# A first stage that reads its features by rows from memory, with wider transfers and paired gate matmuls, in a one-core hybrid mLSTM / mixture-of-experts kernel

## Chip, cores and metric

The kernel runs on one core of a Trainium2 chip. The metric is the device time of one execution in microseconds (us); the time before is a median of three runs. PE is TensorE, DVE is VectorE, ACT is ScalarE, POOL is GpSimd, and SP is SyncE, which here only issues transfers.

## What is computed

One layer on 256 latent tokens and 256 context tokens of width 2048. The part that the change touches is the start of the mixer: LayerNorm, a modulation by shift and scale, and the first columns of the input projection.

```python
cond = silu(concat([c, c_ctx]))                       # two conditioning rows
mod  = cond @ w_ada + b_ada                           # 6 x 2048 for each row
hl = LN(x)   * (1 + scale_l) + shift_l                # latent tokens
hc = LN(ctx) * (1 + scale_c) + shift_c                # context tokens
q, k, v, i, f, o, u, bg, cg = split(hl @ w_in)        # latent: all columns
k, v, i, f of the context   = split(hc @ w_in[:, :state])
# bidirectional chunked mLSTM (context state, then latent) | short gated convolution
x1 = LN(alpha * x + gate * (concat(m, y) @ w_out)) * g1 + b1
# router, 16 SwiGLU experts (top 2), x = LN(alpha * x1 + gate * moe) * g2 + b2
```

## The kernel before

All large weights stream from memory once, in slabs of about 1 MB that SP issues one after another into a rotation of slots (`slab`, L125). A matmul of the mixer is three matmuls (`mm3`, L134): each operand is split into a rounded part (`..._hi`, `wq..h`) and a remainder (`..._lo`, `wq..l`), the rounded part by ACT (L281, L316), the remainder by DVE (L282, L317).

The stages follow one another: (1) the start, in which four row tiles `xrow` (two of the context, two of the latents) are loaded, DVE takes their LayerNorm statistics (`ln_stats`), DVE and ACT norm the rows (L255, L257), and PE transposes them by 128x128 blocks into `xT` (L269, copied out by L270); (2) a loop over 16 feature tiles j (L291) that accumulates q and k of the latents (`qps`, `kps`), k of the context (`kcps`) and the gates (`gps`); (3) the values (`vps`, weights `wv`), during which DVE also reduces 56 slabs `wt` of w_ada against the broadcast conditioning row `cbc` (L424); (4) the mLSTM and its projections, the output projection, the second norm and the router; (5) 16 experts, each with 24 slabs `we` (L909, L937).

In the loop of stage 2, feature tile j needs four numbers for each of its features, `mod`. `modulation(j)` makes them: 16 matmuls `ada` on two 1 MB slabs `wa` (L236), a DVE copy `part` (L239), two small matmuls that add the four partial rows up (L241) and a DVE addition (L244). ACT then makes `hm` = xT * scale + shift (L314, context half and latent half), `hc_hi` and `hl_hi` (L316) and the rounded weights (L281); 18 matmuls of 512 columns follow on PE, and two gate matmuls of 256 columns for this j (L330). The code calls `modulation(j + 2)` in loop j. In j = 10 to 13, 16 matmuls with `condf` against the identity spread the conditioning row over the partitions (L305), and DVE copies it to `cbc` (L307).

The order on each engine is fixed when the program is built: a scheduler takes the instructions of the code above and lists them for each engine, and each engine runs its list in that order, waiting where an operand isn't there.

Of the kernel before, what the change touches and what calls it, by code (L numbers as in the profile page):

```python
# [19 lines left out]
P = 128  # L20
# [35 lines left out]
ROT = 6  # L56
# [40 lines left out]
def tile_layer(ctx: ExitStack, tc: tile.TileContext, x, ctxt, condT, wada01, wadaT, wada5, b5, wqkg, wv, wproj,  # L97
# [9 lines left out]
    ringp = ctx.enter_context(tc.tile_pool(name="ringp", bufs=4))  # L107
# [3 lines left out]
    def mmt(name):  # L111
        return ps.tile([P, 512], F32, tag="mm", bufs=4, name=name)
# [4 lines left out]
    def adt(name):  # L117
        return ps.tile([P, 512], F32, tag="ad", bufs=1, name=name)

    slots = [(ringp, "ring")] * 4  # L120
# [80 lines left out]
    xT = xtp.tile([P, 16, 2 * T], F32, name="xT")  # L201
    rows = []
    for src in (ctxt, x):
        for tt in range(2):
            r = xp.tile([P, D], F32, tag=f"x{len(rows)}", name=f"xrow{len(rows)}")
            nc.sync.dma_start(r, src[tt * P:(tt + 1) * P, :])
            rows.append(r)
    nc.sync.dma_start(cst, consts)
    nc.sync.dma_start(sm, small)
# [10 lines left out]
    mods = {}  # L220
    wqs, was = {}, {}

    def load_ada(j):
        for hf in range(2):
            was[j, hf] = slab(f"wa{j}_{hf}")
            nc.sync.dma_start(was[j, hf], wada01[j, hf])

    def modulation(j):

        pa = adt(f"ada{j}")  # L230
        for hf in range(2):
            ws = was.pop((j, hf))
            wv_ = ws.rearrange("p (a n) -> p a n", a=8)
            for i in range(8):
                g = i % 4
                nc.tensor.matmul(pa[32 * g:32 * g + 32, 0:256], condf[:, hf * 8 + i, :], wv_[:, i, :],  # L236
                                 start=(hf == 0 and i < 4), stop=(hf == 1 and i >= 4), tile_position=(0, 32 * g))
# [8 lines left out]
    def load_qkg(j):  # L246
        wqs[j] = slab(f"wq{j}")
        nc.sync.dma_start(wqs[j][:, 0:1056], wqkg[j])

    load_ada(0)  # L250
    load_qkg(0)
    for i, r in enumerate(rows):
        mv, y, nb = ln_stats([r], f"l0_{i % 2}")
        if i > 1:
            nc.vector.tensor_scalar(r, r, y[:, 0:1], nb[:, 0:1], op0=ALU.mult, op1=ALU.add)  # L255
        else:
            nc.scalar.activation(r, r, AF.Identity, scale=y[:, 0:1], bias=nb[:, 0:1])  # L257

    bias4 = cp.tile([P, 16, 4], F32, name="bias4")
    for i in range(2):  # L260
        nc.vector.tensor_copy(bias4[:, :, i], sm[:, B_ADA:B_ADA + 16])
        nc.vector.tensor_scalar(bias4[:, :, 2 + i], sm[:, B_ADA + 16:B_ADA + 32], 1.0, None, op0=ALU.add)
    modulation(0)
    for i, r in enumerate(rows):
        for b in range(4):
            pt = mmt(f"xT{i}_{b}")
            for q in range(4):
                dt = b * 4 + q
                nc.tensor.transpose(pt[:, q * P:(q + 1) * P], r[:, dt * P:(dt + 1) * P], ident)  # L269
            (nc.vector.tensor_copy if b % 2 else nc.scalar.copy)(  # L270
                xT[:, b * 4:b * 4 + 4, i * P:(i + 1) * P], pt.rearrange("p (q t) -> p q t", q=4))
    load_ada(1)
# [3 lines left out]
    slots = slots + [(xp, f"x{i}") for i in range(4)]  # L276
# [13 lines left out]
    token_tiles(0)  # L290
    for j in range(16):  # L291
        if j + 2 < 16:
            load_ada(j + 2)
        if j + 1 < 16:
            load_qkg(j + 1)
        if j == 5:
            slots = [q for q in slots if q not in early]
            turn[0] = ROT
        if j == 8:
            token_tiles(1)  # L300
        if j in (10, 11, 12, 13):
            cb = adt(f"cb{j}")
            for q in range(4):
                k = (j - 10) * 4 + q
                nc.tensor.matmul(cb[:, q * P:(q + 1) * P], condf[:, k, 0:1].to_broadcast([P, P]), ident,  # L305
                                 start=True, stop=True)
            nc.vector.tensor_copy(cbc[:, (j - 10) * 512:(j - 9) * 512], cb)  # L307
        mod = mods.pop(j)
        wq = wqs.pop(j)
        jj, jt = j // 8, j % 8  # L310
        hm = cp.tile([P, 2, T], F32, tag="modt", bufs=2, name=f"hm{j}")
        for src, hi, lo, k in ((xT[:, j, 0:T], hc_hi, hc_lo, 1), (xT[:, j, T:2 * T], hl_hi, hl_lo, 0)):
# [5 lines left out]
        wh, wl = split(wq[:, 32:1056], [P, 1024], f"wq{j}")  # L318
# [386 lines left out]
    slots = [(endp, "N0"), (endp, "N1"), (endp, "N2"), (post, "W4")] + slots[i:] + slots[:i]  # L705
# [472 lines left out]
def pack(x, c, ctx, c_ctx, w_ada, b_ada, w_in, b_igate, b_fgate, mh_norm_g, conv_w, conv_b, w_out, ln1_g, ln1_b,  # L1178
# [33 lines left out]
    return [x, ctx, condT, wada01, wadaT, wada5, A(b_ada)[:, 10240:11264], wqkg, wv, wproj, wo, w1s, w3s, A(w2)[0], w2l, wrt,  # L1212
# [3 lines left out]
NAMES = ["x", "ctxt", "condT", "wada01", "wadaT", "wada5", "b5", "wqkg", "wv", "wproj", "wout", "w1", "w3", "w2", "w2l", "wrt",  # L1216
# [15 lines left out]
```

## Time and profile before

| | us |
|---|---|
| median of 3 runs | 1570.54 (1570.5 to 1570.57) |
| the profiled execution, its own time | 1572.7 |
| its span, first to last instruction | 1569.4 |
| PE busy in the span | 1435.5 (91%) |
| DVE busy | 557.6 (36%) |
| ACT busy | 347.1 (22%) |
| bytes moved by DMA | 585.52 MB, 373 GB/s on average |

The page lists, for the one profiled execution, each engine's busy time, and groups of equal instructions with the idle time ahead of them and what ended it. The times of single instructions and the waits come from queries of the same trace.

### The profile page before, as it was taken

The page shows a single profiled execution, that of the slowest core. Times are in us where ns is not written, and L with a number is a line of the kernel's source. Part 1 is how long each engine was busy: PE and PEld are TensorE (multiplying, and loading weights), DVE is VectorE, ACT ScalarE, POOL GpSimd, SP SyncE. Part 2 cuts the span into 40 slices and gives each one's busy share as a digit, 9 for nine tenths or more (in the row PEclk, how much of TensorE's full clock was granted, in tenths as well). Part 3 has the DMA queues.
Part 4 walks back from the last instruction along what each step waited for, and adds up shares of the span by engine and source line. Part 5 has one row for each costly group of instructions (what it writes and reads, how often), then busy time and mean ns, then how long its engine had stood idle before and what let it go on. Part 6 is the DMA issues. An engine that isn't in the chain of part 4 may idle for free. (4 is left out here: it accounts for less than half of the span.)

```text
span 1569.4 us, 19076 instructions
## 1 busy us (share of the span) xinstructions
PE 1435.5 (91%) x7917; PEld 800.3 (51%) x7917; DVE 557.6 (36%) x934; ACT 347.1 (22%) x600; POOL 9.7 (1%) x19
## 2 busy tenths in 40 slices
PE   5999999999999989999989989979879979889985
PEld 4666788999998855334324324324324324224331
DVE  6334986988876763110110110101101101101106
ACT  5333325644443342002002002002002002002101
POOL 0000000000000000000000000000000000000001
PEclk9999999999999989999999999999999999999998
DMA  9796796888878897999999999999999999999993
GB/s 393 295 389 266 272 397 238 314 327 324 318 297 325 299 400 306 422 421 422 421 422 421 422 422 421 422 422 421 422 422 421 421 421 422 422 409 413 420 377 134
DMA packets 84081, 585.52 MB, mean 373 GB/s; under 512 B 9636, under 2 KB 10904, under 8 KB 14232
## 3 DMA queue, kind: packets, MB, share of 16 engines
q1 hardware_dynamic: 82088, 579.96, 90.9%
q0 software_dynamic: 432, 3.15, 0.5%
q10 hardware_dynamic: 1472, 1.16, 0.3%
q8 instruction: 63, 1.03, 0.3%
q14 instruction: 26, 0.21, 0.0%
HBM read 582.06 MB, written 2.17 MB: 372 GB/s over the span
## 5 line engine op out<-in xcount | busy, mean ns | idle before, releaser
L909 PE MATMUL h<-we,xg 128*64 128x512 f32 x2048 | 460.2, 597 | 26.8 <-DMA we<-w 26.8
L909 PEld LDWEIGHTS h<-we,xg 128*64 128x64 f32 x2048 | 146.5, 137 | 313.1 <-issue 232.1
L937 PE MATMUL y<-we,aT 128*64 128x512 f32 x960 | 222.2, 600 | 39.4 <-DMA we<-w 28.5
L922 DVE TENSOR_TENSOR act<-act,h 128x512 f32<-128x512 f32 x16 | 11.0, 687 | 542.3 <-PE h L909 542.3
L937 PEld LDWEIGHTS y<-we,aT 128*64 128x64 f32 x960 | 62.3, 136 | 189.7 <-issue 88.5
L424 DVE CUSTOM_DVE_ANT_0 wt<-wt,cbc 128x2048 f32<-128x2048 f32 x56 | 127.3, 2284 | 9.2 <-DMA wt<-wadaT 9.1
L941 DVE TENSOR_TENSOR ysb<-y,g2b 128x512 f32<-128x512 f32 x30 | 20.7, 691 | 262.7 <-PE y L937 262.7
L875 ACT ACTIVATE xg<-gx,modc 128x128 f32<-128x128 f32 x127 | 55.7, 456 | 181.5 <-PE gx L871 178.3
L949 PE MATMUL cb<-ysb,pg 64*128 64x512 f32 x240 | 82.9, 635 | 0.0
L952 DVE TENSOR_TENSOR xl<-xl,cb 128x512 f32<-128x512 f32 x112 | 70.7, 682 | 5.5 <-PE cb L949 5.0
L919 ACT ACTIVATE pg<-pgp 128x256 f32<-128x256 f32 x16 | 6.1, 383 | 270.1 <-PE pgp L916 270.1
L871 PEld LDWEIGHTS gx<-oh,xh 128*128 128x128 f32 x512 | 59.4, 196 | 6.1 <-DVE xl L952 5.3
L871 PE MATMUL gx<-oh,xh 128*128 128x128 f32 x512 | 60.9, 281 | 0.7 <-DVE oh L850 0.7
L949 PEld LDWEIGHTS cb<-ysb,pg 64*128 64x128 f32 x240 | 31.0, 184 | 51.7 <-DVE xl L952 29.0
L927 ACT ACTIVATE aT<-atp 128x512 f32<-128x512 f32 x16 | 9.6, 597 | 214.0 <-PE atp L925 214.0
L921 ACT ACTIVATE act<-h 128x512 f32<-128x512 f32 x16 | 9.6, 597 | 139.1 <-PE h L909 139.1
L314 ACT ACTIVATE hm<-xT,mod 128x256 f32<-128x256 f32 x32 | 17.6, 595 | 74.1 <-DVE mod L244 74.1
L236 PE MATMUL ada<-wa,condf 128*32 128x256 f32 x512 | 31.8, 383 | 0.0
L239 DVE COPY part<-ada 128x256 f32<-128x256 f32 x16 | 6.8, 423 | 61.1 <-PE ada L236 61.1
L282 DVE TENSOR_TENSOR wo_0l<-wo,wo_0h 128x1024 fp32r<-128x1024 f32 x16 | 19.5, 1221 | 14.3 <-ACT wo_0h L281 14.3
L282 DVE TENSOR_TENSOR wo_1l<-wo,wo_1h 128x1024 fp32r<-128x1024 f32 x16 | 19.6, 1223 | 13.4 <-ACT wo_1h L281 13.4
L269 PE MATMUL xT<-cst,xrow 128*128 128x128 f32 x64 | 9.9, 314 | 15.1 <-DMA cst<-consts 14.7
(1123 smaller groups left out, 2221.2 us busy)
## 6 DMA issues: line engine op xcount, KB each, us to landing
we<-w SPq DMA_DIRECT2D x373, 1024.0 KB, 19.8
wt<-wadaT SPq DMA_DIRECT2D x56, 1024.0 KB, 7.1
wa<-wada SPq DMA_DIRECT2D x32, 1024.0 KB, 14.8
wo<-wout SPq DMA_DIRECT2D x16, 1024.0 KB, 7.0
wq<-wqkg SPq DMA_DIRECT2D x16, 528.0 KB, 13.7
wv<-wv SPq DMA_DIRECT2D x8, 1024.0 KB, 7.0
pu<-wproj SPq DMA_DIRECT2D x8, 1024.0 KB, 7.9
pc<-wproj SPq DMA_DIRECT2D x8, 1024.0 KB, 7.0
```

What stands on the lines that cost most here:

```text
L236: nc.tensor.matmul(pa[32 * g:32 * g + 32, 0:256], condf[:, hf * 8 + i, :], wv_[:, i, :], start=(hf == 0 and i < 4), stop=(hf == 1 and i >= ...
L282: nc.vector.tensor_sub(lo, w_ap, hi.bitcast(F32))
L314: nc.scalar.activation(hm[:, 1 - k, :], src, AF.Identity, scale=mod[:, 2 + k:3 + k], bias=mod[:, k:k + 1])
L424: nc.vector.tensor_tensor_reduce(ws, ws, cbc, 1.0, 0.0, ALU.mult, ALU.add, accum_out=adac[:, i:i + 1])
L871: nc.tensor.matmul(gp[:, i * n:(i + 1) * n], xh[t][:, dt * P:(dt + 1) * P], ohs[t], start=(t == 0), stop=(t == 1))
L875: nc.any.tensor_scalar(xg[:, dt, 0:n], gp[:, i * n:(i + 1) * n], sc2[:, dt:dt + 1], sh2[:, dt:dt + 1], op0=ALU.mult, op1=ALU.add)
L909: nc.tensor.matmul(h_[g * 64:g * 64 + 64, :], xs[:, dt, :], ws[:, c0:c0 + 512], start=(dt == 0), stop=(dt == 15), tile_position=(0, 64 * g))
L922: nc.vector.tensor_tensor(act, act, hp[1], op=ALU.mult)
L937: nc.tensor.matmul(yp[i][g * 64:g * 64 + 64, :], half(aT, ft), ws[:, c0:c0 + 512], start=(ft == 0), stop=(ft == 7), tile_position=(0, 64 * g))
L941: nc.vector.tensor_tensor(ysb[:, i * 512:(i + 1) * 512], yp[i], g2b[:, i * 512:(i + 1) * 512], op=ALU.mult)
L949: nc.tensor.matmul(cps, pg[gsl, t, :], ysb[gsl, i * 512:(i + 1) * 512], start=True, stop=True, tile_position=(64 * g, 0))
L952: nc.vector.tensor_tensor(acc[t][:, c0:c0 + 512], acc[t][:, c0:c0 + 512], cps, op=ALU.add)
```

## The change

Stage 1 and the loop of stage 2 are rebuilt; what follows them keeps its code, except for the pools from which its slots come.

- The four row tiles are still loaded, but only for the statistics. The features are loaded a second time in transposed order (`xTs`, four chunks of 1 MB, the first one in two pieces), and the program norms them there: `rnorm` and `bnorm` hold scale and offset of all 512 tokens in every partition (8 matmuls against the identity), and `normalise` multiplies and adds with two DVE instructions for each pair of feature tiles. The 64 transposes, their 16 copies and the four norms by row are gone.
- `wa` comes in 16 transfers of 2 MB into three wide slots, the weights of q and k in eight transfers of 1 MB for two j each (the first one in two halves), the gate columns of all j in one transfer `wg` of 0.26 MB.
- `modulation` is cut in two; in the code, `modulation_sums(j + 2)` (16 matmuls and the copy) stands between the halves t = 0 and t = 1 of the 18 matmuls, and `modulation(j + 2)` behind them.
- The gate matmuls of two j run together at the odd one.
- The conditioning row is loaded broadcast from memory (`crow`, 1 MB) and one ACT instruction applies SiLU; the 16 matmuls and four copies are gone.
- `hm` has three buffers instead of two. The ring of four 1 MB slots is opened behind the loop, in the place of the wide slots; for the experts it is closed and opened again with seven slots, which take the place of the four and of three others.

```diff
+    nc.sync.dma_start(cst, consts)
...
-    early = [(lat, "L1"), (lat, "L3"), (ctxp, "C1"), (ctxp, "C3")]
-    slots = slots + early
+    def load_xT(c):
+        xTc[c] = xtp.tile([P, 4, 2 * T], F32, tag=f"xT{c % 3}", name=f"xT{c}")
+        xv = xTs[c].rearrange("p (k t) -> p k t", k=4)
+        for k in ((0, 1), (1, 4)) if c == 0 else ((0, 4),):
+            nc.sync.dma_start(xTc[c][:, k[0]:k[1], :], xv[:, k[0]:k[1], :])
...
+    wide_slots = [(widep, "wa"), (widep, "wa"), (xp, "xA")]
+    pair_slots = [(lat, "L1"), (lat, "L3"), (ctxp, "C1"), (ctxp, "C3"), (xp, "x2"), (xp, "x3"), (xp, "x2"), (xp, "x3")]
...
-    def modulation(j):
+    def modulation_sums(j):
         pa = adt(f"ada{j}")
+        wv_ = was.pop(j).rearrange("p (a n) -> p a n", a=16)
+        for i in range(16):
+            g = i % 4
+            nc.tensor.matmul(pa[32 * g:32 * g + 32, 0:256], condf[:, i, :], wv_[:, i, :],
+                             start=(i < 4), stop=(i >= 12), tile_position=(0, 32 * g))
...
+    parts[j] = pa, part
+    def modulation(j):
+        pa, part = parts.pop(j)
...
+    rp_, bp_ = mlt("rnormp"), mlt("bnormp")
     for i, r in enumerate(rows):
...
+        for o, col in ((rp_, y), (bp_, nb)):
+            nc.tensor.matmul(o[:, i * P:(i + 1) * P], col[:, 0:1].to_broadcast([P, P]), ident, start=True, stop=True)
...
-                nc.tensor.transpose(pt[:, q * P:(q + 1) * P], r[:, dt * P:(dt + 1) * P], ident)
...
+    def normalise(j0, j1):
+        v = xTc[j0 // 4][:, j0 % 4:j0 % 4 + j1 - j0, :]
+        for row, op in ((rnorm, ALU.mult), (bnorm, ALU.add)):
+            nc.vector.tensor_tensor(v, v, row[:, None, :].to_broadcast([P, j1 - j0, 2 * T]), op=op)
...
     for j in range(16):
+        load_ada(j + 4)
+        if j % 2 == 0:
+            load_qk(j // 2 + 2)
...
+            nc.sync.dma_start(cbc, crow.to_broadcast([P, D]))
...
-        if j in (10, 11, 12, 13):
-            cb = adt(f"cb{j}")
...
+            if t == 0 and j + 2 < 16:
+                modulation_sums(j + 2)
         if j + 2 < 16:
             modulation(j + 2)
...
+        if j % 2:
+            for a in range(2):
+                for k in (j - 1, j):
...
+    wide.close()
+    ring = ExitStack()
+    ringp = ring.enter_context(tc.tile_pool(name="ringp", bufs=4, reuse_waits="tile"))
```

PE of the kernel before, from the last matmuls of j = 3 (`wq3`) to the first of j = 4 (`wq4`):

```order
L136 MATMUL kcps1_343<-wq3l_543,hc_hi0_347 128x512
L137 MATMUL kcps1_343<-wq3h_542,hc_lo0_348 128x512
L236 MATMUL ada5_564<-wa5_0_529,condf_70 32x256 x8
L236 MATMUL ada5_564<-wa5_1_531,condf_70 32x256 x8
L241 MATMUL ada5_564<-cst_69,part5_581 128x2 x2
L330 MATMUL gps_344<-hm4_595,wq4_533 32x256 x2
L135 MATMUL qps0_338<-wq4h_602,hl_hi0_345 128x512
```

The sums `ada5` stand behind the matmuls of j = 3, one whole j ahead of the first reader of `hm5`. PE of the changed kernel, from the last matmuls of j = 4 to the first of j = 5:

```order
L134 MATMUL kcps1_267<-wq4l_522,hc_hi0_271 128x512
L135 MATMUL kcps1_267<-wq4h_521,hc_lo0_272 128x512
L257 MATMUL ada5_474<-wa5_331,condf_67 32x256 x16
L267 MATMUL ada5_474<-cst_66,part5_491 128x2 x2
L366 MATMUL gps_268<-hm5_570,wg_101 32x256
L366 MATMUL gps_268<-hm4_514,wg_101 32x256
L366 MATMUL gps_268<-hm5_570,wg_101 32x256
L133 MATMUL kcps0_266<-wq5h_577,hc_hi0_271 128x512
```

The sums `ada5` have moved behind the matmuls of j = 4, directly ahead of the readers of `hm5`. ACT of the kernel before around the same place:

```order
L314 ACTIVATE hm4_595<-xT_86,mod4_525 128x256 x2
L316 ACTIVATE hc_hi0_347<-hm4_595 128x256
L316 ACTIVATE hl_hi0_345<-hm4_595 128x256
L281 ACTIVATE wq4h_602<-wq4_533 128x1024
L314 ACTIVATE hm5_655<-xT_86,mod5_585 128x256 x2
```

One j is one period of this list. ACT of the changed kernel, j = 4 and 5 (`wq2_275` is the slab of this pair):

```order
L342 ACTIVATE hm4_514<-xT1_122,mod4_447 128x256 x2
L344 ACTIVATE hc_hi0_271<-hm4_514 128x256
L344 ACTIVATE hl_hi0_269<-hm4_514 128x256
L311 ACTIVATE wq4h_521<-wq2_275 128x1024
L311 ACTIVATE wq5h_577<-wq2_275 128x1024
L342 ACTIVATE hm5_570<-xT1_122,mod5_504 128x256 x2
```

The rounded weights of both j of a pair stand behind `hl_hi` of the even one. SP of the kernel before, from the last slab `wa` to the first slabs of the values:

```order
L226 DMA wa15_1_1153<-wada01 128x2048
L248 DMA wq14_1155<-wqkg 128x1056
L248 DMA wq15_1217<-wqkg 128x1056
L445 DMA wv0_0_1372<-wv 128x2048
L423 DMA wt0_1430<-wadaT 128x2048
```

Two slabs of q and k follow the last `wa`. SP of the changed kernel at the same place:

```order
L238 DMA wa14_865<-wada01 128x4096
L249 DMA wq7_867<-wqk 128x2048
L238 DMA wa15_921<-wada01 128x4096
L484 DMA wv0_0_1248<-wv 128x2048
L462 DMA wt0_1306<-wadaT 128x2048
```

`wv0_0` now follows `wa15` directly; its slot lies in the place of a wide slot, and the transfer waits for the sums `ada15` on PE.

## Rows read from the trace of the kernel before

**Rows 1.** The page: the span, and the costliest group with the idle time before it

```profile
span 1569.4 us, 19076 instructions
...
L909 PE MATMUL h<-we,xg 128*64 128x512 f32 x2048 | 460.2, 597 | 26.8 <-DMA we<-w 26.8
```

**Rows 2.** Table of stretches: from:to, length, busy time by engine, granted clock, DMA

```profile
core 0: us, PE busy (x) PEld busy (x) DVE busy (x) ACT busy (x) POOL busy (x), PEclk, DMA share, GB/s
28.40:154.50 126.10, 119.67 (x912) 80.58 (x908) 45.58 (x86) 42.68 (x79) 0.00 (x0) 1.00 0.81 323
154.50:556.00 401.50, 399.60 (x2470) 356.43 (x2471) 319.68 (x446) 175.90 (x262) 0.97 (x6) 1.00 0.82 312
570.00:585.00 15.00, 8.77 (x88) 5.80 (x80) 9.34 (x34) 12.08 (x27) 0.00 (x0) 0.77 0.99 395
600.00:610.00 10.00, 10.00 (x65) 5.83 (x65) 5.78 (x26) 6.21 (x12) 0.00 (x0) 1.00 0.17 43
610.00:1505.00 895.00, 810.47 (x3826) 307.14 (x3824) 106.77 (x165) 78.45 (x167) 1.78 (x3) 1.00 1.01 418
```

**Rows 3.** What PE waited for, 28 to 560: total us, times, longest

```profile
PE ada L241 <- DVE part L239: 5.5, 10, 0.5
PE gtp L406 <- DVE tokt L397: 0.8, 1, 0.8
```

**Rows 4.** Timeline of PE, j = 2 to 3: start, length, instruction, [idle before]

```profile
46.90 0.50 PE L135 MATMUL qps<-wq2h,hl_hi 128*128 128x512 f32 x1
...
51.30 1.93 PE L236 MATMUL ada<-wa,condf 128*32 128x256 f32 x32
53.79 0.61 PE L241 MATMUL ada<-cst,part 128*128 128x2 f32 x4 [0.55 <-DVE part L239]
54.32 0.62 PE L330 MATMUL gps<-hm,wq 128*32 128x256 f32 x4
54.88 0.50 PE L135 MATMUL qps<-wq3h,hl_hi 128*128 128x512 f32 x1
```

**Rows 5.** Timeline of ACT at the same place

```profile
54.63 1.10 ACT L314 ACTIVATE hm<-xT,mod 128x256 f32<-128x256 f32 x2 [5.33 <-DVE mod L244]
55.63 0.40 ACT L316 ACTIVATE hc_hi<-hm 128x256 fp32r<-128x256 f32 x1
55.94 0.40 ACT L316 ACTIVATE hl_hi<-hm 128x256 fp32r<-128x256 f32 x1
56.24 1.05 ACT L281 ACTIVATE wq4h<-wq 128x1024 fp32r<-128x1024 f32 x1
```

**Rows 6.** Timeline of DVE at the same place

```profile
53.31 0.42 DVE L239 COPY part<-ada 128x256 f32<-128x256 f32 x1 [4.47 <-PE ada L236]
54.43 0.16 DVE L244 TENSOR_TENSOR mod<-ada,bias 128x4 f32<-128x4 f32 x1 [0.70 <-PE ada L241]
54.51 1.23 DVE L282 TENSOR_TENSOR wq3l<-wq,wq3h 128x1024 fp32r<-128x1024 f32 x1
```

**Rows 7.** PE where stages begin: j = 0, 10, 14, and the values

```profile
28.46 0.49 PE L135 MATMUL kcps<-wq0h,hc_hi 128*128 128x512 f32 x1
...
110.22 1.16 PE L305 MATMUL cb<-cst,condf 128*128 128x128 f32 x8
...
145.23 0.50 PE L135 MATMUL qps<-wq14h,hl_hi 128*128 128x512 f32 x1
...
155.17 0.50 PE L135 MATMUL vps<-wv_0h,hc_hi 128*128 128x512 f32 x1 [0.70 <-ACT qk_sb L359]
```

**Rows 8.** Timeline of DVE in the start

```profile
5.72 2.47 DVE L178 BATCH_NORM_STATS2 l_0st<-xrow 128x6 f32<-128x512 f32 x4 [5.72 <-DMA xrow<-ctxt]
...
18.65 1.34 DVE L255 TENSOR_SCALAR xrow<-xrow,l_0y,l_0nb 128x2048 f32<-128x2048 f32 x1
...
21.24 0.15 DVE L182 SCALAR_TENSOR_TENSOR l_1nb<-l_1mv,l_1y 128x1 f32<-128x1 f32 x1
```

**Rows 9.** The page's DMA issues: KB each, median us from issue to landing

```profile
wa<-wada SPq DMA_DIRECT2D x32, 1024.0 KB, 14.8
```

More of the change, by code (lines that the diff above doesn't have):

```diff
@@ L199, in token_tiles @@
         hc_lo.append(ctxp.tile([P, 8, T], F32R, tag=f"C{2 + i}", name=f"hc_lo{i}"))
[L201 to L209, printed above, removed]
     splits = ExitStack()
@@ L213, in tile_layer @@
     cbp = splits.enter_context(tc.tile_pool(name="cbp", bufs=1))
-    early = [(lat, "L1"), (lat, "L3"), (ctxp, "C1"), (ctxp, "C3")]
-    slots = slots + early
+    wide = ExitStack()
+    widep = wide.enter_context(tc.tile_pool(name="widep", bufs=2))
+    nc.sync.dma_start(cst, consts)
+    rows = []
+    xA = xp.tile([P, 2, D], F32, tag="xA", name="xrowA")
+    for i, src in enumerate((ctxt, x)):
+        for tt in range(2):
+            r = xA[:, tt, :] if i == 0 else xp.tile([P, D], F32, tag=f"x{2 + tt}", name=f"xrow{2 + tt}")
+            nc.sync.dma_start(r, src[tt * P:(tt + 1) * P, :])
+            rows.append(r)
@@ L219, in tile_layer @@
+    nc.sync.dma_start(sm, small)
+    xTc = {}
+    def load_xT(c):
[3 more added lines that the diff above has]
+            nc.sync.dma_start(xTc[c][:, k[0]:k[1], :], xv[:, k[0]:k[1], :])
+    wg = xtp.tile([P, 16, 32], F32, name="wg")
+    rnorm = xtp.tile([P, 2 * T], F32, name="rnorm")
+    bnorm = xtp.tile([P, 2 * T], F32, name="bnorm")
     nc.scalar.activation(condf[:, :, 0:2], cT, AF.Silu)
-    mods = {}
+    mods, parts = {}, {}
@@ L221, in tile_layer @@
     wqs, was = {}, {}
+    wide_slots = [(widep, "wa"), (widep, "wa"), (xp, "xA")]
+    pair_slots = [(lat, "L1"), (lat, "L3"), (ctxp, "C1"), (ctxp, "C3"), (xp, "x2"), (xp, "x3"), (xp, "x2"), (xp, "x3")]
     def load_ada(j):
-        for hf in range(2):
-            was[j, hf] = slab(f"wa{j}_{hf}")
-            nc.sync.dma_start(was[j, hf], wada01[j, hf])
-    def modulation(j):
-        pa = adt(f"ada{j}")
[L231 to L237, printed above, removed]
+        if j < 16:
+            pool, tag = wide_slots[j % 3]
+            was[j] = pool.tile([P, 2 * D], F32, tag=tag, name=f"wa{j}")
+            nc.sync.dma_start(was[j], wada01[j])
@@ L244, in modulation @@
         nc.vector.tensor_tensor(mods[j], pa[:, 0:4], bias4[:, j, :], op=ALU.add)
-    def load_qkg(j):
-        wqs[j] = slab(f"wq{j}")
-        nc.sync.dma_start(wqs[j][:, 0:1056], wqkg[j])
     load_ada(0)
-    load_qkg(0)
-    for i, r in enumerate(rows):
[L253 to L257, printed above, removed]
+    load_xT(0)
+    load_qk(0)
+    nc.sync.dma_start(wg, wgate)
+    load_ada(1)
+    load_ada(2)
+    load_qk(1)
+    load_ada(3)
+    load_xT(1)
+    rp_, bp_ = mlt("rnormp"), mlt("bnormp")
+    for i, r in enumerate(rows):
+        mv, y, nb = ln_stats([r], f"l0_{i}")
+        for o, col in ((rp_, y), (bp_, nb)):
+            nc.tensor.matmul(o[:, i * P:(i + 1) * P], col[:, 0:1].to_broadcast([P, P]), ident, start=True, stop=True)
+    nc.scalar.copy(rnorm, rp_)
+    nc.vector.tensor_copy(bnorm, bp_)
     bias4 = cp.tile([P, 16, 4], F32, name="bias4")
@@ L262, in tile_layer @@
         nc.vector.tensor_scalar(bias4[:, :, 2 + i], sm[:, B_ADA + 16:B_ADA + 32], 1.0, None, op0=ALU.add)
+    modulation_sums(0)
     modulation(0)
[L264 to L268, printed above, removed]
[L269 to L272 removed]
+    def normalise(j0, j1):
+        v = xTc[j0 // 4][:, j0 % 4:j0 % 4 + j1 - j0, :]
+        for row, op in ((rnorm, ALU.mult), (bnorm, ALU.add)):
+            nc.vector.tensor_tensor(v, v, row[:, None, :].to_broadcast([P, j1 - j0, 2 * T]), op=op)
+    normalise(0, 1)
+    modulation_sums(1)
     modulation(1)
     cbc = cbp.tile([P, D], F32, name="cbc")
[L276 removed]
     def split(w_ap, shape, name):
@@ L290, in tile_layer @@
     token_tiles(0)
+    hms = {}
     for j in range(16):
[L292 to L295, printed above, removed]
+        load_ada(j + 4)
+        if j % 2 == 0:
+            load_qk(j // 2 + 2)
+        if j == 1:
+            load_xT(2)
+        if j == 3:
+            nc.sync.dma_start(cbc, crow.to_broadcast([P, D]))
         if j == 5:
-            slots = [q for q in slots if q not in early]
-            turn[0] = ROT
+            load_xT(3)
         if j == 8:
             token_tiles(1)
-        if j in (10, 11, 12, 13):
-            cb = adt(f"cb{j}")
[L303 to L307, printed above, removed]
+            nc.scalar.activation(cbc, cbc, AF.Silu)
         mod = mods.pop(j)
-        wq = wqs.pop(j)
+        wq = wqs[j // 2][:, (j % 2) * 1024:(j % 2) * 1024 + 1024]
         jj, jt = j // 8, j % 8
-        hm = cp.tile([P, 2, T], F32, tag="modt", bufs=2, name=f"hm{j}")
-        for src, hi, lo, k in ((xT[:, j, 0:T], hc_hi, hc_lo, 1), (xT[:, j, T:2 * T], hl_hi, hl_lo, 0)):
+        hm = hms[j] = xtp.tile([P, 2, T], F32, tag="modt", bufs=3, name=f"hm{j}")
+        xj = xTc[j // 4][:, j % 4, :]
+        for src, hi, lo, k in ((xj[:, 0:T], hc_hi, hc_lo, 1), (xj[:, T:2 * T], hl_hi, hl_lo, 0)):
             h_ = hi[jj][:, jt, :]
@@ L317, in tile_layer @@
             nc.vector.tensor_sub(lo[jj][:, jt, :], hm[:, 1 - k, :], h_.bitcast(F32))
-        wh, wl = split(wq[:, 32:1056], [P, 1024], f"wq{j}")
+        wh, wl = split(wq, [P, 1024], f"wq{j}")
+        if j == 0:
+            normalise(1, 2)
+        elif j % 2 and j < 15:
+            normalise(j + 1, j + 3)
         st, en = (j == 0), (j == 15)
```

40 lines of the change are left out of this document (25 added, 15 removed).

## The prediction

> **What bounds the kernel now.** I read the page first. The costliest group, the matmuls of the experts, idles 26.8 us and all of it for its weight slabs [rows 1]; the table of stretches shows the same for 610 to 1505: a DMA share of 1.01 at 418 GB/s [rows 2]. That part is bound by transfers, starts when the first expert's slots begin to come free, and isn't changed. Ahead of it DMA isn't the bound: 0.81 and 0.82 of its time up to 556, and 0.17 between 600 and 610, where all slots are full and wait for the first expert [rows 2]. So what counts is when PE reaches the experts. Between 28.4 and 556 PE runs nearly without a gap: 399.60 of 401.50 us behind the loop [rows 2], and in all of it the waits for other engines are 5.5 us for `part` and 0.8 us for `tokt`, with hardly anything else [rows 3]. A shift of the end of the loop over j therefore passes to the end of the kernel nearly one to one. The question is how long start and loop last: the values begin at 155.17 [rows 7].
>
> **The period of one j before.** In the timeline of PE, j = 2 begins at 46.90, its 18 matmuls end where `ada` begins at 51.30 (4.40 us), 16 sums of j + 2 (L236) take 1.93, L241 starts at 53.79, the gates at 54.32, j = 3 at 54.88 [rows 4]: 7.98 us. From 46.90 to 110.22 [rows 4, 7] eight periods take 63.32, 7.92 each. The chain of `mod` costs PE only the 0.55 us wait for `part`, since `hm` of j + 1 was made one period earlier.
>
> **The change part by part.** The terms are shifts of the moment at which the values begin.
>
> *Lookahead.* The code still asks for the sums of j + 2 in loop j, but in the order as built the sums of j + 1 stand behind the matmuls of j, directly ahead of those of j + 1 (the piece with `ada5` in the section on the change). So PE runs `ada`, then waits for the whole chain. From the start A of `ada`: 2.01 to the copy (51.30 to 53.31), 0.48 to L241, 0.64 to the addition (54.43), 0.20 to `hm` (54.63), 1.00 to `hc_hi` (55.63) [rows 4 to 6]. An odd j begins with the context: `hc_hi` takes 0.40 more, with about 0.05 for the hand-over (an estimate of mine from the gaps between L244 and `hm`), and the gates of the pair, ready when `hm` ends, push it to about A + 4.9. An even j begins with the latents and with weights that ACT rounds only behind `hl_hi`: 1.00 + 0.31 + 0.30 + 1.05 [rows 5] after the start of `hm`, A + 6.05. With 4.40 us ahead of A the two periods are 9.3 and 10.45, 19.75 for a pair against 15.83. From S2 (start of j = 2) to j = 10 that is 79.0, less 0.2 because `ada3` stands one matmul before the end: 78.8 - 63.3 = **+15.5**.
>
> *j = 10 to 13.* Here two sums, `ada12` and `ada14`, stand in the middle of the 18 matmuls, nine earlier (2.2 us), and the first of them finds its weights rounded earlier. I get 9.3, 7.4, 9.3 and 8.55, 34.55 us. Before, this stretch ran from 110.22 to 145.23 [rows 7], 35.01, as it contains the 16 matmuls L305 (0.9 us of the path per j: the first group stands from 110.22, 1.16 us long [rows 7]). The removal of L305 is thus in this term: **-0.4**.
>
> *j = 14 and 15.* Before, no sums are left: 145.23 to 155.17, 9.94 [rows 7]. After, `ada15` stands one matmul before the end of j = 14, so 9.05 + 4.4 = 13.4: **+3.5**.
>
> *Start.* 64 transposes, 16 copies and four norms by row go. They matter little: DVE's statistics, bound by the landing of rows, set the start; they run from 5.72 to the last offset at 21.24 [rows 8], with a norm by row of 1.34 [rows 8] and copies of 0.7 between them, which go. After, `cst` (0.5 MB, 1.2 us at 0.42 MB/us) is loaded first, so I put the last offset at 20, `rnorm` and `bnorm` at 21.3, the first `normalise` at 22.7, `mod` of j = 0 at 24.0, the first rounded weights at 26.7, j = 0 at 26.75 against 28.46 [rows 7]. With the chains of j = 1 and 2 (for j = 2 the sums stand in the middle) I reach S2 at 45.3 against 46.90 [rows 4]: **-1.6**, bounds -4 (if the norms and copies that leave DVE shorten the chain behind the last offset too) and +1 (if j = 0 waits for its 2 MB slab).
>
> *Normalise, transfers, `crow`.* DVE has room for the two instructions per pair of features: it is busy 45.58 of 126.10 us in the loop [rows 2], and a multiply of 128x1024 takes about 1.23 like the remainder of `wq` [rows 6]; four of them stand between `mod` and the remainders of odd j, where they end about as PE needs `hc_lo` at its seventh matmul. I take 0, at most +1. The loop's bytes grow from some 47 to 52 MB; at the 418 GB/s of the experts' stretch [rows 2] this is 125 us, and the loop will last 145, so no term. A 1 MB slab landed 14.8 us after its issue in the median [rows 9]; a 2 MB slab is issued three j, about 29 us, ahead of its use. `crow` is off the path.
>
> The Trainium skill, page "DMA: Bandwidth & Descriptors", section "Bandwidth", measures 341 GB/s for 1 MB and 425 for 16 MB, by which 2 MB transfers should be worth something. Rows 2 speak against a gain: a stream of 1 MB slabs already moves 418 GB/s, and the term stays 0 by the one and by the other, as the loop doesn't wait for its slabs.
>
> *Behind the loop.* `wv0_0` waits on SP for `ada15` and everything of that queue waits behind it. By my times `ada15` ends 7 us before the loop, the slab lands 5 us later and its first half is split 3 us after that, about as PE asks for it behind `igp` and `fgp`. So DVE starts the values with the work behind it that was done ahead before. The transposes of `tokt`, for which PE already waited 0.8 us [rows 3], stand one group of twelve matmuls (2.9 us) earlier in the list. Bounds 0 and +5, I take **+1.5**. The order of transfers between the output projection and the experts is changed too; the 8.3 us of idle DMA between 600 and 610 [rows 2] cover it. I take 0, bounds -1 and +2.
>
> **Sum.** -1.6 + 15.5 - 0.4 + 3.5 + 1.5 = +18.5. The profiled execution took 1572.7, of which 1569.4 is the span [rows 1]: 1591.2. The median lies 2.2 below the profiled execution: **1589.0**.
>
> **The rivals.** *The sums are hidden and it gets faster.* If PE stays fed, in that the hand-over from `mod` to the first matmul is shorter than I add up or the chain overlaps with more of the 18 matmuls than the list shows, what remains is the gain: L305 with 0.9 us in four j (-3.6), the waits for `part` (-5.5 [rows 3]), the start (-1.6 to -4) against +1.5 behind the loop: about -10, 1560. It decides where a pair of j takes less than 15.83 us. For it speaks only that ACT has idle time in each period; against it the list itself, since PE can't pass a matmul that waits. *A smaller loss.* If ACT has rounded the weights of even j before they are asked for, an even j begins at A + 5.1 (`hl_hi` ends 0.40 after its start [rows 5]), 0.95 less in seven j; with the start at its bound of -4 that makes 1589 - 6.6 - 2.4 = 1580. ACT's idle 5.33 us of each period [rows 5] would have room for it; its list, with these weights behind `hl_hi`, speaks against it. *The clock falls in the gaps.* Between 570 and 585 PE is busy 8.77 of 15 us and the granted clock is 0.77; in the loop it is 1.00 with 119.67 of 126.10 [rows 2]. After, PE would be busy some 120 of 145 us with a gap of 2 to 3 us in each j. If a tenth of the loop ran at the lower level, 1.2 GHz instead of 2.4, PE would lose half of that tenth, 7 us; if a fifth, 14: 1596 to 1603. The Trainium skill, page "TensorE: Matmul & The Clock Gate", section "Why this matters for your kernels", warns of idle gaps between bursts of matmuls; by it this would be the likelier case. This trace has shown the fall only where PE is idle for four tenths, and the loop will be idle for less than two, so I leave it a small chance. *Values stalled.* DVE, late by some 5 us, holds up PE in the values, +5 more: 1594. *No change.* The gain of the first rival and a loss of that size cancel.
>
> **How the numbers follow.** My forecast 0.62, the clock 0.10, the values 0.08, a smaller loss 0.07, faster 0.10, no change 0.03. This kernel's runs tell about 0.2%, 3.1 us, from no change. Slower: 0.62 + 0.10 + 0.08 + 0.07 = 0.87; same 0.03; faster 0.10. The range reaches from the smaller loss, with some spread, to the middle of the clock's case: 1576 to 1601; the forecast's own bounds (start -2.4 to +2.6, normalise to +1, values -1.5 to +3.5, transition -1 to +2) give 1584 to 1598.
>
> **What would show it.** Right: PE's waits in the loop grow from 6 us to 30 or more, put down to `hm`, `hc_hi` or `wq..h` on ACT, with `ada` directly ahead; starts of j alternate by about 9.3 and 10.4; the values start near 172; the experts' stretch keeps its length. The start is wrong if j = 0 doesn't begin between 25 and 28.5. Wrong: pairs of j below 17 us, a DMA named as what ends PE's waits in the loop, or a granted clock below 0.95 there.

## The result, and the profile after

The changed kernel takes 1616.78 us (median of four runs, 1611.71 to 1619.21) against 1570.55 of the kernel before beside it: a ratio of 1.0286, 95% interval 1.0256 to 1.0317. It is slower, as predicted, but by 46 us where 18.5 were forecast, and beyond the upper end of the range (1601). The profiled execution is the slowest of the four, 1619.21, so the tables below add up to a little more than the ratio: its span is 48.0 us longer.

From the page of the changed kernel, its span and the experts' group of [rows 1]:

```profile
span 1617.4 us, 18869 instructions
...
L949 PE MATMUL h<-we,xg 128*64 128x512 f32 x2048 | 459.7, 596 | 26.2 <-DMA we<-w 26.2
```

The experts' matmuls still idle 26 us for their slabs, as before: nothing is lost or won there. The table of stretches, to be held against [rows 2], where the loop stood at a clock of 1.00:

```profile
core 0: us, PE busy (x) PEld busy (x) DVE busy (x) ACT busy (x) POOL busy (x), PEclk, DMA share, GB/s
28.00:196.00 168.00, 142.79 (x893) 92.14 (x894) 57.63 (x98) 46.58 (x84) 0.67 (x5) 0.85 0.68 264
30.00:90.00 60.00, 52.37 (x340) 33.48 (x342) 23.38 (x35) 12.56 (x25) 0.00 (x0) 0.87 0.91 368
90.00:150.00 60.00, 48.53 (x284) 32.30 (x276) 18.27 (x30) 17.39 (x28) 0.00 (x0) 0.77 0.61 228
150.00:196.00 46.00, 41.23 (x282) 25.80 (x274) 13.98 (x29) 14.63 (x28) 0.67 (x5) 0.93 0.45 169
```

The loop lasts 168 us instead of 126. PE is busy for 143 of them where it was busy for 120 before, although the table counts slightly fewer matmuls in it (893 against 912). So there are two losses, time in which PE waits and time in which it works slowly, and the DMA share has fallen with them. What PE waited for between 28 and 200, the first rows (compare [rows 3]):

```profile
PE gps L366 <- ACT hm L342: 10.7, 12, 0.9
PE ada L267 <- DVE part L260: 5.5, 10, 0.5
```

The timeline of PE shows both losses, first around the beginning of j = 5, then up to that of j = 6 (to be held against [rows 4]):

```profile
77.57 1.93 PE L257 MATMUL ada<-wa,condf 128*32 128x256 f32 x32
80.05 0.61 PE L267 MATMUL ada<-cst,part 128*128 128x2 f32 x4 [0.55 <-DVE part L260]
81.54 1.11 PE L366 MATMUL gps<-hm,wg 128*32 128x256 f32 x6 [0.89 <-ACT hm L342]
...
82.59 0.52 PE L133 MATMUL kcps<-wq5h,hc_hi 128*128 128x512 f32 x1
...
83.33 0.63 PE L133 MATMUL qps<-wq5h,hl_hi 128*128 128x512 f32 x1
83.76 0.63 PE L134 MATMUL qps<-wq5l,hl_hi 128*128 128x512 f32 x1
...
86.57 0.39 PE L134 MATMUL qps<-wq5l,hl_hi 128*128 128x512 f32 x1
86.80 0.39 PE L135 MATMUL qps<-wq5h,hl_lo 128*128 128x512 f32 x1
...
88.53 1.93 PE L257 MATMUL ada<-wa,condf 128*32 128x256 f32 x32
...
92.51 0.62 PE L366 MATMUL gps<-hm,wg 128*32 128x256 f32 x2 [0.89 <-ACT hm L342]
...
94.56 0.80 PE L133 MATMUL qps<-wq6h,hl_hi 128*128 128x512 f32 x1 [1.43 <-ACT wq6h L311]
```

The first loss is the chain: behind the sums `ada`, PE waits 0.55 us for `part`, 0.89 for `hm`, and in j = 4, 6, 8 and 10 another 1.4 for the rounded weights. The second is the clock. Behind such a chain the matmuls of 512 columns start 0.43 us apart (83.33 to 83.76); some 3 us later they start 0.23 apart (86.57 to 86.80). The granted clock of the same stretches (third column from the right) shows the two levels, 2.4 GHz in the chain, 1.2 GHz for the slow matmuls and 2.4 GHz again for the fast ones:

```profile
80.00:82.50 2.50, 1.56 (x10) 0.80 (x10) 1.81 (x3) 1.61 (x4) 0.00 (x0) 1.00 0.81 210
83.30:84.60 1.30, 1.30 (x4) 0.99 (x3) 1.30 (x3) 0.00 (x0) 0.00 (x0) 0.50 1.02 429
86.50:88.50 2.00, 2.00 (x9) 1.34 (x8) 0.00 (x0) 0.00 (x0) 0.00 (x0) 1.00 1.00 422
```

Before the fall PE did nothing but the chain, about 5 us with the sums, the gates and the gaps between them. Of the 263 distances between starts of neighbouring matmuls of this kind in the loop, 85 are long (0.38 to 0.5 us), where the kernel before has none. As a measure of the loss, take all distances of 0.25 to 0.5 us, of which the kernel before has some too: their excess over 0.2335 us, the usual short distance, sums to 18.9 us, against 1.9 before.

Where the 48.0 us arise, from the starts on PE in both timelines (us):

| moment on PE | before | after | added by then | added in this step |
|---|---|---|---|---|
| j = 2 begins | 46.90 | 51.99 | 5.1 | 5.1 |
| j = 10 begins | 110.22 | 142.26 | 32.0 | 27.0 |
| j = 14 begins | 145.23 | 182.33 | 37.1 | 5.1 |
| first instruction behind the loop | 155.17 | 195.92 | 40.8 | 3.7 |
| output projection | 467.18 | 511.09 | 43.9 | 3.2 |
| first expert | 603.65 | 651.93 | 48.3 | 4.4 |
| end of the span | 1569.4 | 1617.4 | 48.0 | -0.3 |

### The profile page after: what moved, and what is told of

Read it like the earlier page. It is cut to its first block, busy times and chain, and to the rows that moved or that the text cites. A ratio compares the mean times of both kernels' runs of the same rounds, so it can differ in the third digit from the quotient of the medians.

```text
span 1617.4 us, 18869 instructions
## 1 busy us (share of the span) xinstructions
PE 1457.4 (90%) x7837; PEld 809.2 (50%) x7837; DVE 567.7 (35%) x940; ACT 340.5 (21%) x592; POOL 9.7 (1%) x19
## 5 line engine op out<-in xcount | busy, mean ns | idle before, releaser
L366 PE MATMUL gps<-hm,wg 128*32 128x256 f32 x64 | 14.8, 418 | 10.7 <-ACT hm L342 10.7
```

What stands on the lines that cost most here:

```text
L366: nc.tensor.matmul(gps[r0:r0 + 32, 0:T], wg[:, k, :], hms[k][:, a, :], start=(k < 2), stop=(k >= 14), tile_position=(0, r0))
```

## Experiments

The theory, once the trace was read: the order on PE, in which the sums of j + 1 stand right behind the matmuls of j, costs the chain and, through the gaps, the clock; the rebuilt stage itself is worth a little. The rivals: that the low clock is a companion that costs nothing of its own; that something else of the rebuilt stage (the features normed in place, the wide transfers, the paired gates) makes the loop long; and that the 2 MB transfers are where its gain lies.

### The order put back by hand: look2

Each `order` fixes behind which instruction another stands on its engine, without adding a wait. The sums of j + 2 stand between the halves of the matmuls of j, as the code of the change reads.

```diff
+            with ExitStack() as order:
+                if t == 1 and j + 2 < 16:
+                    order.enter_context(tc.issue_after(sums[j + 2]))
+                elif j:
+                    order.enter_context(tc.issue_after(sums["mm"]))
                 mm3(qps[t], ...)
...
             if t == 0 and j + 2 < 16:
-                modulation_sums(j + 2)
+                with tc.issue_after(sums["mm"]):
+                    modulation_sums(j + 2)
         if j + 2 < 16:
-            modulation(j + 2)
+            with tc.issue_after(sums["mm"]):
+                modulation(j + 2)
```

> The changed kernel with its PE order set by hand: the sums of j + 2 stand between the halves of j's 18 matmuls, and the first half of j + 1 behind the second half of j, so hm of j + 1 is made a period ahead, as before the change. Theory (the lost lookahead on PE, with the clock that falls in its gaps, is the whole loss): starts of j come back to about 7.9 to 8.0 us, the granted clock in the loop to 1.00, the values start at 150 to 156, and the time is 1555 to 1575. Rival (2 MB transfers, DVE's normalise or the pools behind the loop are to blame): still over 1595, with waits in the loop for other things.

Measured: 1567.58 us, ratio 0.997 (0.9961 to 0.998). The same rebuilt stage is thus 49 us faster by its order alone, and slightly faster than the kernel before. Its timeline in j = 4, and its loop in the table of stretches:

```profile
64.48 0.48 PE L134 MATMUL qps<-wq4h,hl_hi 128*128 128x512 f32 x1
...
67.44 1.93 PE L258 MATMUL ada<-wa,condf 128*32 128x256 f32 x32
69.31 0.50 PE L134 MATMUL qps<-wq4h,hl_hi 128*128 128x512 f32 x1
...
71.51 0.50 PE L269 MATMUL ada<-cst,part 128*128 128x2 f32 x4
71.87 0.48 PE L134 MATMUL qps<-wq5h,hl_hi 128*128 128x512 f32 x1
```

```profile
60.00:148.00 88.00, 87.00 (x670) 60.70 (x671) 40.80 (x69) 35.45 (x61) 0.66 (x5) 1.00 0.90 377
```

One j takes 7.39 us (64.48 to 71.87). It took 7.98 before: the copy `part` now runs beside nine matmuls, so PE no longer waits 0.55 us for it in each j. The expected period, 7.9 to 8.0, had not taken this out. The values begin at 147.26, ahead of the 150 to 156 expected and 7.9 us earlier than before the change; at the first expert 3.8 of these are left (599.9 against 603.65).

### The chain without the change: late

The kernel before, with nothing changed but the place of the sums: j + 1 behind the matmuls of j, instead of j + 2.

```diff
-        if j + 2 < 16:
-            modulation(j + 2)
+        if 0 < j < 15:
+            with tc.issue_after(sums["mm"]):
+                modulation(j + 1)
```

> The kernel before with one thing changed: the sums of j + 1, not of j + 2, stand behind the matmuls of j, for j from 1 on. Transfers, transpositions, gates and pools stay as before. Theory (the place of the sums alone makes the loss): periods of 9.2 us at full clock and more with the clock falling, 25 to 45 us slower than before. Rival (the rest of the change makes it): within 10 us of before.

Measured: 1600.51 us, 1.0177 (1.0156 to 1.0197), 29 us more than before. The old stage loses in the same way as the new one when the lookahead is taken from it, so features by rows, wide transfers and paired gates aren't what makes the loop long. Its timeline between j = 3 and 4, and its loop:

```profile
63.96 1.93 PE L237 MATMUL ada<-wa,condf 128*32 128x256 f32 x32
66.44 0.61 PE L242 MATMUL ada<-cst,part 128*128 128x2 f32 x4 [0.55 <-DVE part L240]
67.93 1.55 PE L332 MATMUL gps<-hm,wq 128*32 128x256 f32 x4 [0.89 <-ACT hm L315]
...
70.01 0.63 PE L137 MATMUL kcps<-wq4l,hc_hi 128*128 128x512 f32 x1
70.43 0.63 PE L136 MATMUL qps<-wq4h,hl_hi 128*128 128x512 f32 x1
```

```profile
40.00:128.00 88.00, 75.55 (x515) 47.50 (x513) 22.01 (x43) 22.09 (x41) 0.00 (x0) 0.92 0.66 257
```

The same 0.55 and 0.89 us, and the same matmuls 0.42 us apart behind them. The clock falls here too, but less (0.92, against 0.84 in the changed kernel from 40 to 128), and the loss is smaller. A part of it has another cause: ahead of j = 14 PE waits 2.99 us for `part`, which DVE makes late there.

### Does the clock cost anything of its own? behind, behind_fill, nofill2, fill2

In behind, the sums of j + 1 are put by hand behind all 18 matmuls of j; behind_fill adds two or three matmuls of 256 columns per j, in the gap behind L267, that write unused columns of `ada`.

```diff
+        if j > 1:
+            for q in range(2 if j % 2 else 3):
+                nc.tensor.matmul(pa[:, 256:512], part[:, 0:P], part, start=True, stop=True)
```

> The changed kernel with the sums of j + 1 put behind all 18 matmuls of j for every j from 1 on, by hand; it is the reference for the run with filler matmuls. At full clock each j would take about 9.3 us and the time would be 1580 to 1588. Theory (the clock falls in the gaps): granted clock 0.75 to 0.9 in the loop, periods of 11 to 12 us, time 1605 to 1625. Rival (the clock of the changed kernel fell for another reason than these gaps): periods near 9.3, 1580 to 1590.

> The same order, and behind the two small matmuls of each modulation two (odd j) or three (even j) matmuls of 256 columns that write unused columns of the same tile, in the time in which PE waits for hm. Theory (what the loop loses beyond the chain is the clock, and filled gaps keep it up): granted clock 0.95 or more in the loop, periods 9.3 to 9.8, and 12 to 25 us less than the run without them. Rival (the loss is waiting, not clock): the same time or up to 5 us more, clock as without.

Measured: behind 1611.04 (1.025, 1.0232 to 1.0268), behind_fill 1621.52 (1.0313, 1.0295 to 1.0331). The time of behind lies where the theory put it, but its periods of 9.7 to 10.6 us lie between the 9.3 of a full clock and the 11 to 12 of the theory. The expected gain of the filling didn't come. The stretch from 62 to 128 of behind and then of behind_fill, and the end of a gap in behind_fill:

```profile
62.00:128.00 66.00, 55.14 (x363) 35.40 (x362) 26.22 (x42) 21.08 (x35) 0.00 (x0) 0.90 0.78 299
```

```profile
62.00:128.00 66.00, 55.97 (x390) 35.61 (x389) 26.30 (x42) 21.64 (x37) 0.00 (x0) 1.00 0.76 288
...
89.62 1.93 PE L258 MATMUL ada<-wa,condf 128*32 128x256 f32 x32
...
92.57 1.54 PE L273 MATMUL ada<-part 128*128 128x256 f32 x6
95.00 0.62 PE L372 MATMUL gps<-hm,wg 128*32 128x256 f32 x2 [0.89 <-ACT hm L347]
```

The filling does hold the clock, at 1.00 instead of 0.90. But the fillers write the tile that the addition `mod` reads, so `mod` waits for them: the gates stand 5.38 us behind `ada` (89.62 to 95.00), where behind has 4.32. The gap grew by more than the clock gave back (the values begin 6.1 us later), and the pair settles nothing.

So it was tried again with fillers that add zeros to the gates' sums, which `mod` doesn't read. nofill2 is behind with the gates of the pair ahead of the sums and DVE's order fixed; fill2 has the same order on every engine and the fillers besides.

```diff
+        if j > 2:
+            for q in range(2 if j % 2 else 3):
+                nc.tensor.matmul(later["gps"][:, 0:T], wg[:, 0, 16:17].to_broadcast([P, P]), part, start=False, stop=False)
```

> The changed kernel with the sums of j + 1 behind all 18 matmuls of j, the gates of a pair ahead of them, and DVE's order fixed so that nothing stands between part and mod except one norm in some j; the reference for the run with fillers. Without a fall of the clock a period would be 9.2 to 9.4 us, with it 10.0 to 10.8. Both theories expect 1600 to 1615 here, the clock theory with a granted clock of 0.85 to 0.95 in the loop.

> The same order on every engine; added are only two or three matmuls of 256 columns behind the two small ones of each modulation from j = 3 on. They add zeros to the sums of the gates, so mod doesn't wait for them as it did in the first run with fillers. Theory (the clock takes what the chain doesn't): granted clock 0.97 or more in the loop, periods of 9.2 to 9.6, 8 to 18 us less than without. Rival (waiting alone costs the time): periods and time within 3 us of the run without.

Measured: nofill2 1616.41 (1.0284, 1.0267 to 1.0301), just above the 1600 to 1615 expected, and fill2 1610.43 (1.0242, 1.0225 to 1.0259): 6.0 us less with more work, somewhat under the 8 to 18 expected. The stretch 62 to 128, the beginning of j = 5, and `igp`, which stands behind the loop and the first matmuls of the values, without fillers and then with them:

```profile
62.00:128.00 66.00, 51.80 (x362) 36.28 (x363) 24.48 (x40) 21.36 (x36) 0.00 (x0) 0.90 0.79 304
...
82.56 0.79 PE L134 MATMUL kcps<-wq5h,hc_hi 128*128 128x512 f32 x1 [2.03 <-ACT hc_hi L350]
83.16 0.63 PE L135 MATMUL kcps<-wq5l,hc_hi 128*128 128x512 f32 x1
83.58 0.63 PE L134 MATMUL qps<-wq5h,hl_hi 128*128 128x512 f32 x1
...
195.78 1.07 PE L399 MATMUL igp<-gT,cst 128*64 128x512 f32 x2
```

```profile
62.00:128.00 66.00, 58.48 (x438) 39.89 (x438) 24.82 (x41) 21.21 (x35) 0.00 (x0) 0.97 0.81 311
...
78.91 1.11 PE L278 MATMUL gps<-part,wg 128*128 128x256 f32 x4
81.07 0.50 PE L134 MATMUL kcps<-wq5h,hc_hi 128*128 128x512 f32 x1 [1.06 <-ACT hc_hi L353]
81.41 0.40 PE L135 MATMUL kcps<-wq5l,hc_hi 128*128 128x512 f32 x1
81.65 0.40 PE L134 MATMUL qps<-wq5h,hl_hi 128*128 128x512 f32 x1
...
185.83 1.07 PE L402 MATMUL igp<-gT,cst 128*64 128x512 f32 x2
```

Without fillers the clock falls in about every second period: the periods of odd j from 3 on take 10.9 to 11.15 us, most of the even ones 9.2 to 9.5. With the gap filled, the matmuls of j = 5 start 0.24 us apart instead of 0.42 (81.41 to 81.65, 83.16 to 83.58), and the long periods fall to 9.6, except those of j = 9 and 11, which stay at 11.15. `igp` begins at 185.83 instead of 195.78, 9.95 us earlier. The lower clock thus costs time of its own, and the count of the long distances tells how much: 75 with 15.7 us in nofill2, 32 with 7.7 us in fill2, 8.0 apart. Not all of the 10 us arrived at the end: the first expert was reached 7.0 us earlier, and from there to the last `y` the experts took 949.1 us instead of 944.3. Of these 4.8 us, 3.0 are a longer wait of PE ahead of `g2q`: 6.3 and 2.8 us in fill2, 6.1 in nofill2. The first pair shows the same, 5.8 and 4.5 us in behind_fill and 6.1 in behind. The work there is the same; why the wait is longer in the runs with fillers wasn't tried. The two profiled executions, from which these moments come, are only 2.3 us apart; the medians are 6.0 apart.

### What the order is worth in the old stage: before_mid

The kernel before, its sums of j + 2 put between the halves as in look2.

```diff
+            if t == 0 and j + 2 < 16:
+                with tc.issue_after(sums["mm"]):
+                    modulation_sums(j + 2)
...
-            modulation(j + 2)
+            with tc.issue_after(sums["mm"]):
+                modulation(j + 2)
```

> The kernel before with one thing changed: the sums of j + 2 stand between the halves of j's matmuls, and the first half of j + 1 behind the second half of j. Theory (the gain of the run with lookahead comes from the order, which hides the wait for part, and not from the rebuilt stage): periods of 7.4 instead of 7.98 for j below 10, the values 5 to 9 us earlier, the time 1562 to 1567. Rival (the gain is that of the rebuilt stage): within 2 us of before.

Measured: 1575.79 us, 1.0021 (1.0011 to 1.0031): slightly slower, where 1562 to 1567 were expected. The periods from j = 2 on are about as short as expected (7.47 to 7.89) until a slab is missing; then j = 6 takes 15.33 us. PE in that place, the stretch ahead of it, and the queue of SP:

```profile
85.23 3.64 PE L237 MATMUL ada<-wa,condf 128*32 128x256 f32 x32 [4.89 <-DMA wa<-wada]
...
75.00:80.00 5.00, 5.00 (x28) 3.23 (x26) 1.98 (x5) 2.66 (x5) 0.00 (x0) 1.00 0.00 0
...
55.41 25.75 SPq L227 DMA_DIRECT2D wa<-wada  x3
```

From 75 to 80 nothing is transferred: SP needs 25.75 us for three slabs `wa`, and all behind them waits; 18.0 of it SP waits for DVE's `wq6l`, that is for a slot of the shared rotation. With the old slots the better order alone gains nothing here; in look2, where `wa` has slots of its own, PE is busy for 87.00 of the 88 us shown. That these slots are the reason is argued, as no run gave them to the old stage. The prediction hadn't seen this use of the rebuilding.

### Where the gain of the rebuilt stage lies: look2_slots, ls_base, ls_small, ls_cb, ls_wq0

look2_slots is look2 with a different order of slots for the eight slabs `w` of the second gate, which precede the experts; ls_base is the same code again, beside its three variants.

```diff
-    slots = ([(morep, "M0")] + [(ringp, "ring")] * 4 + [(ctxp, f"C{i}") for i in (2, 3, 0, 1)])
+    slots = ([(morep, "M0")] + [(ctxp, f"C{i}") for i in (2, 3, 0, 1)] + [(ringp, "ring")] * 4)
```

> The run with the lookahead restored, with one line changed: the eight slabs of the second gate (w5) take the four slots of the context pool ahead of the ring's four, which come free only when the output projection ends. Theory (the ring that is opened again behind the output projection makes w5 late, which costs 3 to 4 us between the output projection and the first expert): PE's waits for w5 go and the time falls 1 to 4 us against the run with lookahead, to 1563 to 1567. Rival (the experts' stream sets that time anyway): within 1 us of it.

> The kernel with the lookahead restored and w5 in the context pool's slots first, once more, as the base of the three that follow. 1563 to 1567, or 0.995 to 0.998 of before.

Measured: look2_slots 1566.62 (0.9963, 0.9949 to 0.9977), ls_base 1565.46 (0.9961, 0.9947 to 0.9975). The first expert begins 2.2 us earlier than in look2 (597.7 against 599.9), yet PE still waits for these slabs ahead of it (3.1 us, 2.6 in look2), against the expectation, and the interval holds look2's ratio: whether the slots help isn't settled. With ls_small below it is the fastest version of the case, some 6 us faster than the kernel before.

The wide transfers, halved:

```diff
-            nc.sync.dma_start(was[j], wada01[j])
+            for hf in range(2):
+                nc.sync.dma_start(was[j][:, hf * D:hf * D + D], wada01[j][:, hf * D:hf * D + D])
```

> That kernel with each 2 MB slab of w_ada in two transfers of 1 MB into the same slot. Theory (the size of these transfers is worth nothing, since the loop doesn't wait for them): within 1.5 us of the base. Rival (2 MB transfers move faster): 2 us or more over the base, with waits for wa in the loop.

Measured: 1565.34 us, 0.9958 (0.9945 to 0.9972), the same as ls_base within what these runs can tell. The size of the transfers is worth nothing here.

The conditioning row by 16 matmuls again, instead of a load from memory:

```diff
-            nc.sync.dma_start(cbc, crow.to_broadcast([P, D]))
...
+        if j in (10, 11, 12, 13):
+            cb = adt(f"cb{j}")
+            for q in range(4):
+                k = (j - 10) * 4 + q
+                nc.tensor.matmul(cb[:, q * P:(q + 1) * P], condf[:, k, 0:1].to_broadcast([P, P]), ident,
+                                 start=True, stop=True)
+            nc.vector.tensor_copy(cbc[:, (j - 10) * 512:(j - 9) * 512], cb)
```

> That kernel with the conditioning row spread by 16 matmuls and four copies in j = 10 to 13, as before the change, and without its transfer and its SiLU on ACT. Theory (these matmuls stand on PE's path): periods of j = 10 to 13 longer by 0.9 to 1.2, the values 3.5 to 4.8 us later, the time 2 to 4.5 us over the base. Rival (the gain is given back behind the loop): within 1 us.

Measured: 1567.83 us, 0.9976 (0.9967 to 0.9985), 2.4 us over ls_base, as expected, though the two intervals overlap. The values begin 1.75 us later, less than the 3.5 to 4.8 expected: the periods of j = 10 to 13 are 0.45 to 0.9 us longer instead of 0.9 to 1.2, and ls_cb was 1.0 us ahead when j = 10 began.

The weights of j = 0 rounded ahead of `hm`, to take away the wait of 2.9 us for `wq0h`:

```diff
+                if j == 0:
+                    order.enter_context(tc.issue_after(later[0]))
```

> That kernel with the weights of j = 0 rounded ahead of its hm on ACT; in the base PE waits 2.9 us for them. If they have landed by then: j = 0 starts 0.5 to 1.5 us earlier and the time falls by up to 1.5 us. If they land later than mod, ACT is held up and nothing is won.

Measured: 1566.64 us, 0.9967 (0.9955 to 0.998), no gain. PE begins j = 0 at 27.58 instead of 29.67, and its third matmul waits for the remainder from DVE:

```profile
30.76 0.79 PE L135 MATMUL qps<-wq0l,hl_hi 128*128 128x512 f32 x1 [1.95 <-DVE wq0l L314]
```

The wait changed its name and stayed.

## Why the prediction was wrong

**The chain: right.** From the start of `ada` the prediction put `hm` at 3.33 us and the first matmul of an even j at 6.05; measured in j = 6, the latter is 6.03 (88.53 to 94.56). The odd j = 5 begins 5.02 behind its `ada` (77.57 to 82.59), forecast 4.9. The first two periods from j = 2, in which the clock still held, are 9.20 and 10.43, forecast 9.3 and 10.45. PE's waits in the loop are those that were named, 26.5 us in all where 30 or more were given as the sign.

**The clock: the step that failed.** The prediction had it as a rival with a chance of 0.10 and a price of 7 to 14 us. The forecast put this cost at nothing. From j = 4 to 11 the periods are 11 to 12 us, and the lookahead term is 27.0 instead of 15.5; the stretch j = 10 to 13 gives +5.1 instead of -0.4 (its own figures, 34.55 less 35.01, make -0.46). The values begin at 197.78 instead of 172, and the clock of 0.85 in the loop is below the 0.95 that the prediction had named as a sign of being wrong. Up to the end of the loop the forecast's terms are +17.0 and the measurement +40.8; of the 23.8 us between them the long distances of the matmuls account for 17.0 (18.9 less 1.9): 2.3 ahead of j = 2, 10.2 up to j = 10, 4.4 in j = 10 to 13 and 0.1 behind. This share is worked out from the trace; that a loss of this kind is the clock's, and of this size per long distance, fill2 against nofill2 shows. The reason given for the small chance, that the trace had shown the fall only where PE is idle for four tenths [rows 2], took one stretch for a limit. Here the clock was 0.77 with PE busy for 48.5 of 60 us, and since a slow matmul counts as longer busy, that share hides the very gaps that were to be judged.

The Trainium skill, page "TensorE: Matmul & The Clock Gate", section "Why this matters for your kernels", warns of idle gaps between bursts of matmuls, but it speaks of gaps longer than those that the prediction worked out. So it did not make the fall the likelier case, as the prediction read it. The trace of after goes beyond the page: behind j = 0 its longest wait is 1.43 us, and yet the clock fell to 0.77 in the stretch from 90 to 150.

**The start: wrong in sign.** -1.6 was forecast, +5.1 came. j = 0 began at 29.35, outside the 25 to 28.5 that were given as the test. Three rows of after bear on it, the second of them from the table of stretches:

```profile
21.82 3.43 PE L257 MATMUL ada<-wa,condf 128*32 128x256 f32 x32
...
21.80:25.30 3.50, 3.45 (x33) 1.39 (x32) 1.98 (x3) 0.28 (x1) 0.00 (x0) 1.00 1.06 432
...
29.35 0.79 PE L133 MATMUL qps<-wq0h,hl_hi 128*128 128x512 f32 x1 [2.94 <-ACT wq0h L311]
```

The sums took 3.43 us instead of 1.93, and the first rounded weights came behind `hl_hi` on ACT; so j = 0 began 2.6 us behind its forecast of 26.75. The pace of the sums is near that of the lower level (3.64 us in before_mid, at a granted clock of 0.50 from 85.2 to 88.8), but the profile grants 1.00 here, so why they were slow stays open. From j = 0 to j = 2 another 4.1 us went missing, 2.3 of them in the long distances above. The transposes that the change took away had been hidden beside DVE's statistics, and PE had been busy with them; that this work held the clock up is argued, not shown.

**j = 14 and 15: right**, +3.7 for +3.5. **Behind the loop: nearly right** up to the output projection, +3.2 for +1.5 with the bound at +5; a wait of 2.0 us for `wv_0h` and a granted clock of 0.83 between 235 and 245 lie in it. **The transition: wrong**, +4.4 for 0, above the bound of +2. One of its waits is not among those of the kernel before, for slabs that the idle DMA of [rows 2] was to cover:

```profile
PE ada L723 <- DMA w<-wada: 3.4, 2, 1.9
```

It stays in look2 (2.6 us) and look2_slots (3.1 us); what of the rest belongs to the order of slots isn't settled.

**No term for the transfers: right.** None of PE's waits in the loop of after names a transfer, and ls_small shows it with the order put back. **The rival of a faster kernel** named what the rebuilt stage would be worth if PE stayed fed: about -10. With the order put back it is -3.6 in look2 and -6 in ls_base, whose slots for the second gate's slabs stand in another order: the waits for `part` and the removed matmuls are there, the earlier start isn't.

Left open is why the sums came to stand behind the matmuls as built, though the code asks for them between the halves. No run tried it; look2 only fixes the order by hand.

## What to carry to other kernels

Price a gap on the tensor engine twice, for itself and for the matmuls behind it at the lower clock, and where gaps come in every period of a loop, as here, give the fallen clock more than a small chance even if each gap is short. Read the order as built rather than the code, and fix by hand the few places on which the lookahead rests: here this is the difference between 1.0286 and 0.997 for the same stage. A busy share can't show such a loss, since slow work counts as busy; the distance between equal instructions does.

## What the hardware showed that was not expected

- The clock fell though no single gap behind j = 0 was longer than 1.5 us: in j = 4 to 11 of after, PE idles 0.55 and 0.89 us, in even j also 1.43, with small matmuls between them, and six to eleven of the distances between the matmuls behind them are 0.43 us. Behind the gaps ahead of j = 2 and 3 it held. Matmuls of 256 columns in part of such gaps raised the clock of the stretch from 0.90 to 0.97 or 1.00.
- Work added to PE made the kernel 6.0 us faster (fill2 against nofill2), although its output is the same.
- Fillers in unused columns of a tile delayed that tile's reader: `mod` of j = 6 waited for them in behind_fill, and the gates moved from 4.32 to 5.38 us behind `ada`.
- The same work of the experts took 944.3 us in nofill2 and 949.1 and 950.3 in the two runs with fillers, which wait 3.0 and 4.2 us longer ahead of `g2q`. The cause is open.
